# First modulation by column blocks of 1 MB behind x; four q chunks projected chunk by chunk of the tokens in four PSUM banks

## The chip, the core and the metric

The kernel runs on one core of a Trainium2 chip. The core has TensorE (PE in the profile) for matrix products into the accumulation memory PSUM, VectorE (DVE) and ScalarE (ACT) for elementwise work, GpSimd (POOL) and SyncE (SP); each takes its instructions in the order in which they stand, and an instruction that waits holds up everything behind it on its engine. Transfers are issued from a queue of SP, ACT or POOL and are moved by 16 DMA engines that all queues share. The metric is the device time of one execution in microseconds (us), the median of several.

## The reference

One layer of a hybrid diffusion block on 1024 latent tokens and 256 context tokens of width 1024, all in fp32. What this change touches is its beginning: the modulation from the condition `c`, the normed and modulated tokens `h`, and the input projection.

```python
mod = jax.nn.silu(c) @ w_ada[i] + b_ada[i]          # (1, 6 * 1024)
mod_c = jax.nn.silu(c_ctx) @ w_ada[i] + b_ada[i]
sh1, sc1, g1, sh2, sc2, g2 = jnp.split(mod[:, None, :], N_MOD, axis=-1)
hc = modulate(rmsnorm(xc, norm1_g[i]), csh1, csc1)   # x * (1 + scale) + shift
k_c, v_c = jnp.split(hc @ w_in[i][:, NA_WIDTH:3 * NA_WIDTH], 2, axis=-1)
h = modulate(rmsnorm(x, norm1_g[i]), sh1, sc1)
q, k, v, hv, hx1, hx2, gna, ghy = jnp.split(h @ w_in[i], IN_SPLITS, axis=-1)
```

Behind it stand neighbourhood attention on q, k, v (8 heads), a long convolution on hv, hx1, hx2 (with filters from a small sine network), gates, an output projection, and a SwiGLU network; they aren't changed.

## The kernel before

**Products.** An fp32 operand is split into a high part (the value rounded to the fast matmul type, one cast on ACT, line 174) and a low part (the rest, one subtraction on DVE, line 175). A product is then three matmuls: low by high, high by low, high by high (line 194).

**The input projection.** `w_in` has 40 chunks of 128 output columns: 0 to 3 are q, 4 to 7 k, 8 to 11 v, 12 to 23 the convolution's inputs, 24 to 39 the gates. A chunk is projected for two halves of 512 tokens; a half takes 8 contraction chunks by three matmuls, 24 in all, into one PSUM bank (`in_ps`). Chunks 4 to 11 also have a product with the 256 context tokens (`ctx_ps`). `project` is a generator that does one chunk at a time; a priority pulls the next chunk's weights ahead.

**The start** (`hidden`). The first 2048 columns of `w_ada`, 8 MB, are loaded as 8 blocks of 1 MB, each with 128 contraction rows of all columns, in three buffers; every block adds to one accumulation (`ada_ps`, line 299), so that shift and scale are known only when the last block is in. The first four token tiles (x, 128 tokens by 1024) are loaded between the blocks. Their squares are summed on ACT (line 280), the root is taken (line 239), the tiles are scaled (lines 287 and 289), turned on PE (`hT_ps`, line 248), modulated alternately on ACT (line 262) and DVE (line 259) into `htmp`, and split into `hTh` and `hTl`. Tiles 4 to 7 make the second half, the two context tiles `hcTh` and `hcTl`. `filter_hidden` is the sine network (`mlp_ps`, line 338; `farg`, `fkf`, lines 339 to 344; the sine on ACT, line 345), in two layers that stand beside all this.

**What follows.** Three generators are merged by fixed shares: `side` (the filters, lines 350 to 397, then the convolutions) and `proj`, until `side` ends. Then five chunks are projected, and the remaining ones stand between the 32 steps of the attention, one half (24 matmuls) per step; when none is left, `hyena_out` gives 12 matmuls (`hy_ps`) to a step, 16 times. A step is scores (`s_ps`), softmax on DVE and ACT, transposes and the product with v (`pt_ps`), copied out by ACT. The order of all engines' instructions is set when the program is built, by a scheduler that follows priorities and its own estimate of time; lines marked `keep_in_program_order` stay in written order.

These are the lines of the start that set the order:

```python
for k in range(8):
    w = pool.tile([P, 2048], F32, tag="wada", name="wada", bufs=3)
    nc.sync.dma_start(w, a["w_ada"][k, :, 0:2048])
    ...
    if 1 <= k < 5:
        load(k - 1)
    if k == 5:
        normed(0, 4, "rstd1")
```

## Time and profile before

| | |
|---|---|
| time, median of 3 runs | 1698.57 us (1697.81 to 1703.14) |
| the profiled execution's own time | 1693.98 us |
| its span, first to last instruction | 1691.6 us |
| DVE, ACT, POOL busy | 1229.1, 689.6, 153.3 us |
| HBM read and written | 205.48 and 67.39 MB, 161 GB/s over the span |
| granted TensorE clock, mean | 0.994 |

The profile has a page with the busy time of each engine, and views that answer questions on the trace: the timeline (start, duration, engine, line, operation, output<-inputs, number of instructions merged, and in brackets the idle time before it and what ended it) and windows (busy time of each engine in a stretch, then the granted clock, the DMA engines' share and GB/s). Line numbers in them are those of the kernel before. A matmul's shown duration runs to its modelled end; in a row of equal ones the distance from start to start is what one costs. An fp32 product shows as two records.

### The profile page before, as it was taken

What the parts mean: (1) busy time and instruction counts of PE and PEld (TensorE: products, weight loads), DVE (VectorE), ACT (ScalarE), POOL (GpSimd) and SP (SyncE); (2) the same over time, 40 slices, a digit from 0 to 9 for tenths busy, and PEclk for the clock granted to TensorE, in tenths of its full rate; (3) what the DMA queues carried; (4) which work ended last, traced back from release to release, by engine and by line L of the source; (5) the groups of instructions that cost most, each with busy time, mean ns of one, the idle gap of its engine ahead of it and who ended that gap; (6) DMA issues with size and microseconds to landing.
All of it is one profiled execution on the core that took longest, in us unless ns stands there. A gap on an engine that the chain in (4) does not pass through costs nothing.

```text
span 1691.6 us, 22631 instructions
## 1 busy us (share of the span) xinstructions
PE 1645.8 (97%) x8124; PEld 1302.7 (77%) x8124; DVE 1229.1 (73%) x2076; ACT 689.6 (41%) x1206; POOL 153.3 (9%) x274
## 2 busy tenths in 40 slices
PE   6999999999999999999999999999999999999997
PEld 2777667777777787887787887888888888878886
DVE  3799587799986975565866867967865666489467
ACT  4733333222212124545654326733333334355455
POOL 0100210001000022020200001000100111000000
PEclk8999999999999999999999999999999999999999
DMA  9275662655544366344757414333422223395344
GB/s 363 96 241 194 193 215 81 209 168 172 185 169 178 124 204 182 110 140 147 218 159 256 162 62 174 119 129 121 162 92 108 94 102 123 113 359 188 100 119 155
DMA packets 110340, 274.36 MB, mean 162 GB/s; under 512 B 15503, under 2 KB 24595, under 8 KB 107925
## 3 DMA queue, kind: packets, MB, share of 16 engines
q1 hardware_dynamic: 90152, 211.86, 37.3%
q0 software_dynamic: 19280, 60.60, 10.7%
q8 instruction: 64, 1.05, 0.3%
q10 hardware_dynamic: 797, 0.45, 0.1%
q14 instruction: 47, 0.39, 0.1%
HBM read 205.48 MB, written 67.39 MB: 161 GB/s over the span
## 4 chain that ended last, share of the span: by engine, by line
PE 68%; issue 11%; DVE 5%; DMA 3%; ACT 1%; POOL 1%; SPq 0%; DVEq 0%; POOLq 0%; ACTq 0%
PE x_ps L1176 15%; PE in_ps L194 13%; PE z_ps L1176 7%; PE dx_ps L1345 6%; PE out_ps L1114 4%; PE dz_ps L1345 3%; PE dft_ps L447 2%; PE hy_ps L194 2%; PE y_ps L1176 2%; PE pt_ps L805 2%; PE pt_ps L791 2%; PE na_ps L194 2%; PE dy_ps L1345 1%; PE dft_ps L448 1%; PE dft_ps L449 1%
## 5 line engine op out<-in xcount | busy, mean ns | idle before, releaser
L194 PE MATMUL in_ps<-hTh,wl 128*128 128x512 f32 x640 | 258.4, 404 | 0.9 <-ACT proj L619 0.5
L194 PE MATMUL in_ps<-hTl,wh 128*128 128x512 f32 x640 | 252.2, 394 | 0.4 <-DVE hTl L175 0.2
L194 PE MATMUL in_ps<-hTh,wh 128*128 128x512 f32 x640 | 252.2, 394 | 0.0
L194 PEld LDWEIGHTS in_ps<-hTh,wl 128*128 128x128 f32 x640 | 120.5, 188 | 31.3 <-issue 5.3
L194 PEld LDWEIGHTS in_ps<-hTl,wh 128*128 128x128 f32 x640 | 120.6, 188 | 26.5 <-DVE hTl L175 1.9
L194 PEld LDWEIGHTS in_ps<-hTh,wh 128*128 128x128 f32 x640 | 120.5, 188 | 26.6
L175 DVE TENSOR_TENSOR wl<-wr,wh 128x1024 fp32r<-128x1024 f32 (+1 forms) x56 | 59.7, 1067 | 68.4 <-ACT wh L174 68.2
L174 ACT CAST wh<-wr 128x1024 fp32r<-128x1024 f32 (+1 forms) x56 | 51.8, 925 | 139.9 <-PE in_ps L194 112.2
L175 DVE TENSOR_TENSOR ol<-ws,oh 128x512 fp32r<-128x512 f32 x88 | 60.4, 688 | 49.1 <-ACT oh L174 49.0
L175 DVE TENSOR_TENSOR ol<-ar,oh 128x512 fp32r<-128x512 f32 x77 | 52.8, 688 | 48.0 <-ACT oh L174 48.0
L174 ACT CAST oh<-ar 128x512 fp32r<-128x512 f32 x77 | 47.9, 622 | 87.1 <-PE dx_ps L1345 33.1
L174 ACT CAST oh<-ws 128x512 fp32r<-128x512 f32 x88 | 54.7, 622 | 55.7 <-PE x_ps L1176 22.1
L780 ACT ACTIVATE pe<-pe,mx 128x640 f32<-128x640 f32 x64 | 52.6, 823 | 48.7 <-DVE mx L779 48.7
L447 PE MATMUL dft_ps<-a,matf 128*128 128x512 f32 x128 | 66.2, 598 | 4.9 <-issue 2.3
L779 DVE CUSTOM_DVE_ANT_0 pe<-s_ps,bias 128x640 f32<-128x640 f32 x64 | 50.1, 820 | 28.3 <-PE s_ps L774 28.2
L1345 PE MATMUL dx_ps<-ol,oh 128*128 128x512 f32 x176 | 68.7, 390 | 1.7 <-DVE ol L175 1.7
L1345 PE MATMUL dx_ps<-oh,ol 128*128 128x512 f32 x176 | 67.4, 390 | 1.9 <-DVE ol L175 1.9
L1345 PE MATMUL dx_ps<-oh 128*128 128x512 f32 x176 | 68.5, 389 | 0.0
L174 ACT CAST oh<-wr 128x512 fp32r<-128x512 f32 x70 | 43.3, 621 | 51.3 <-PE x_ps L1176 15.5
L175 DVE TENSOR_TENSOR ol<-wr,oh 128x512 fp32r<-128x512 f32 x70 | 48.0, 688 | 22.0 <-ACT oh L174 21.9
L1116 DVE TENSOR_TENSOR x<-x,out_ps 128x512 f32<-128x512 f32 x64 | 42.7, 684 | 16.9 <-PE out_ps L1114 16.7
L895 DVE SCALAR_TENSOR_TENSOR aacc<-wal,cs,aacc 128x512 f32<-128x512 f32 x56 | 41.8, 746 | 17.5 <-DMA wal<-in_w_ada 16.9
(396 smaller groups left out, 4215.8 us busy)
## 6 DMA issues: line engine op xcount, KB each, us to landing
wr<-in_w SPq DMA_DIRECT2D x52, 512.0 KB, 3.4
wr<-in_w_in SPq DMA_DIRECT2D x40, 512.0 KB, 4.4
ar<-g SPq DMA_DIRECT2D x77, 256.0 KB, 3.2
wal<-in_w_ada SPq DMA_DIRECT2D x64, 256.0 KB, 4.1
matf<-in_dft_f SPq DMA_DIRECT2D x32, 384.0 KB, 4.9
bias<-in_rpb SPq DMA_DIRECT2D x64, 192.0 KB, 3.7
g<-t POOLq DMA_DIRECT2D x47, 256.0 KB, 3.1
w<-in_w SPq DMA_DIRECT2D x44, 256.0 KB, 5.4
```

The costliest lines, as they stand in the source:

```text
L174: self.nc.scalar.copy(hi, src)
L175: self.nc.vector.tensor_sub(lo, src, hi.bitcast(F32))
L194: mm = nc.tensor.matmul(ps, ww[:, k * P:(k + 1) * P], xx[:, k, pos:pos + width], start=(i == 0), stop=(i == n - 1))
L447: nc.tensor.matmul(ps, m[:, 0], v.rearrange("p a b -> p (a b)"), start=True, stop=False)
L779: nc.vector.tensor_tensor_reduce(pe, ps[:, 256:896], bt, -1.0, 3e38, ALU.add, ALU.min, mx[:, 0:1])
L780: nc.scalar.activation(pe, pe, AF.Exp, bias=mx[:, 0:1], scale=-1.0, accum_out=mx[:, 1:2])
L791: pin(nc.tensor.transpose(pt[:, at:at + P], pe[:, c * P:(c + 1) * P], self.ident))
L895: nc.vector.scalar_tensor_tensor(acc, w, c, acc, op0=ALU.mult, op1=ALU.add)
L1114: nc.tensor.matmul(ps, gg[x][:, tk], ww[y][:, sl], start=(i == 0), stop=(i == n - 1))
L1116: nc.vector.tensor_add(x1[:, sl], x1[:, sl], ps)
L1176: mm = nc.tensor.matmul(ps, w[u][:, k * P:(k + 1) * P], x[v][:, k, :], start=(start and k == 0 and i == 0), stop=(stop and k == 3 and i == 2),
L1345: nc.tensor.matmul(ps[j], x[u][:, j * P:(j + 1) * P], w[v], start=(start and i == 0 and c == 0), stop=(stop and i == N - 1 and k == len(re ...
```

## The change

`w_ada1` is a second copy of the first 2048 columns, laid out as 8 column blocks of 1 MB: block k has all contraction rows of the 128 shift and the 128 scale columns of chunk k, so one block alone gives shift and scale of that chunk. The four x tiles are loaded first; then come block 0, the weights of q chunk 0, block 1, q chunk 1, and so on, four blocks ahead in the memory of `hT[1]`, all in written order. Each block has 8 small-column matmuls, a copy of 256 columns to SBUF, two matmuls of two columns with a selecting matrix `sel` in place of the transposes, and two small DVE operations. The projection opens with the q chunks 0 to 3, which were 20th to 23rd before: when contraction chunk k of the first half is there, the q chunks add their three matmuls of it, each in its own PSUM bank; q chunk n joins when k reaches n and catches up. The second half goes likewise. Then come 4, 5 and the rest. `left`, which counts the chunks until the last, goes from 40 to 36.

```diff
+    out["w_ada1"] = C(A("w_ada")[0, :, :2 * D].reshape(8, P, 2, 8, P).transpose(3, 1, 0, 2, 4)).reshape(8, P, 2048)
...
-        self.left = 40
+        self.left = 36
...
+    def ada_block(self, pool, psf, w, k, cs, sel):
+        ps = psf.tile([P, 512], F32, tag="f", name="ada_ps")
+        for n in range(8):
+            j = n % 4
+            nc.tensor.matmul(ps[32 * j:32 * j + 32, 0:256], cs[:, n], w[:, n], start=(n < 4), stop=(n >= 4),
+                             tile_position=(0, 32 * j))
+        b = pool.tile([P, 256], F32, tag="msb", name="msb", bufs=2)
+        nc.vector.tensor_copy(b, ps[:, 0:256])
+        for n in range(2):
+            nc.tensor.matmul(ps[:, 256 + 2 * n:258 + 2 * n], b[:, n * P:(n + 1) * P], sel, start=True, stop=True)
...
+        for j in range(4):
+            load(j)
+        for k in range(4):
+            block(k)
+            raws[k] = pool.tile([P, D], F32, tag="x", name="wr", bufs=8)
+            inorder(nc.sync.dma_start(raws[k], a["w_in"][group[k]]))
+        normed(0, 4, "rstd1")
+        turns = [self.turned(psf, xs[0:4], 0)]
         for k in range(8):
...
+            self.ada_block(pool, psf, blocks[k], k, cs, sel)
+            if 1 <= k <= 4:
+                block(k + 3)
+            if k < 7:
+                turns.append(self.turned(psf, xs[0:4], k + 1))
+            self.chunk(pool, turns[k], 4, self.mod1[:, 0], *hT[0], k)
...
+            if k == 6:
+                for j in range(4, 10):
+                    inorder(load(j))
...
         normed(4, 4, "rstd1b")
...
+        for k in range(8):
+            self.chunk(pool, self.turned(psf, xs[4:8], k), 4, self.mod1[:, 0], *hT[1], k)
+            if k == 7:
+                normed(8, 2, "rstd1c")
+            yield
...
+        def opening(group, sts):
+            for h in range(2):
+                banks = [p.tile([P, 512], F32, tag=t, name="in_ps") for p, t in
+                         ((psg[0], "g"), (psg[1], "g"), (psc, "c"), (psf, "f"))]
+                for k in range(8):
+                    next(between)
+                    for n, f in enumerate(group):
+                        if n > k and not h:
+                            continue
+                        wh, wl = self.ready[f]
+                        for kk in (range(k + 1) if n == k and not h else (k,)):
+                            for i, (ww, xx) in enumerate(((wl, 0), (wh, 1), (wh, 0))):
+                                nc.tensor.matmul(banks[n], ww[:, kk * P:(kk + 1) * P], hT[h][xx][:, kk, :],
+                                                 start=(kk == i == 0), stop=(kk == 7 and i == 2))
+                for f, st, pt in zip(group, sts, banks):
+                    out(f, st, [pt], h)
...
-                order = [[4, 5]] + [[f] for f in list(range(6, 24)) + list(range(4)) + list(range(32, 40)) + list(range(24, 30))]
+                order = [list(range(4))] + [[f] for f in list(range(4, 24)) + list(range(32, 40)) + list(range(24, 30))]
```

What the scheduler made of it shows at three places. The first is DVE at the start: `farg` and `fkf` are the sine network, `rstd` the reciprocal that scales x. Before:

```order
L342 SCALAR_TENSOR_TENSOR farg<-fkf,farg 128x1024
L343 SCALAR_TENSOR_TENSOR farg<-fkf,farg 128x1024
L344 TENSOR_SCALAR farg<-farg 128x1024
L241 RECIPROCAL rstd_371<-rstd1s 128x4
L289 TENSOR_SCALAR x<-x,rstd_371 128x1024 x2
```

And now:

```order
L277 TENSOR_REDUCE sel<-ident 128x2
L366 TENSOR_SCALAR fkf<-farg 128x1024
L367 TENSOR_SCALAR fkf<-fkf 128x1024
L368 SCALAR_TENSOR_TENSOR farg<-fkf,farg 128x1024
L369 SCALAR_TENSOR_TENSOR farg<-fkf,farg 128x1024
L242 RECIPROCAL rstd_359<-rstd1s 128x4
L370 TENSOR_SCALAR farg<-farg 128x1024
L296 TENSOR_SCALAR x<-x,rstd_359 128x1024 x2
```

The reciprocal still stands behind the sine network's four long operations; x itself now comes first in the queue of transfers.

The second place is ACT between the two token halves (with buffer numbers; `junk` is the squares of x, here of tiles 4 to 7, `proj` the copies of the finished q chunks out of PSUM):

```order
L265 ACTIVATE htmp_628<-hT_ps_587,mod1_246 128x512
L174 CAST hTh_260<-htmp_628 128x512
L174 CAST hTh_260<-htmp_672 128x512
L287 ACTIVATE junk_676,ssq1_298<-x_632 128x1024
L287 ACTIVATE junk_678,ssq1_298<-x_634 128x1024
L626 ACTIVATE proj_290<-in_ps_294 128x512
L287 ACTIVATE junk_680,ssq1_298<-x_636 128x1024
L626 ACTIVATE proj_291<-in_ps_295 128x512
L287 ACTIVATE junk_682,ssq1_298<-x_638 128x1024
L626 ACTIVATE proj_292<-in_ps_296 128x512
L240 ACT_TABLE_LOAD
L240 ACTIVATE rstd1bs_684<-ssq1_298,eps_236 128x4
```

The first half's last cast (chunk 7) stands ahead of the squares of tiles 4 to 7, as before, where only the cast of one chunk's weights and one copy stood with them; now there are three copies among them.

The third place is PE at the end of the attention (line 826 scores, 846 transposes, 860 the product with v). The last `hy_ps` group now ends like this:

```order
L196 MATMUL hy_ps<-yhh,wh 128x512
L826 MATMUL s_ps<-krh,qrl 128x384 x2
L826 MATMUL s_ps<-krl,qrh 128x384 x2
L826 MATMUL s_ps<-krh,qrh 128x384 x2
L829 MATMUL s_ps<-kch,ql 128x256 x2
L829 MATMUL s_ps<-kcl,qh 128x256 x2
L829 MATMUL s_ps<-kch,qh 128x256 x2
L846 MATMUL pt_ps<-ident,pe 128x128 x10
L860 MATMUL pt_ps<-pts,vc 64x128 x4
L860 MATMUL pt_ps<-pts,v 64x128 x6
```

and before like this:

```order
L194 MATMUL hy_ps<-yhh,wh 128x512
L791 MATMUL pt_ps<-ident,pe 128x128 x10
L805 MATMUL pt_ps<-pts,vc 64x128 x4
L805 MATMUL pt_ps<-pts,v 64x128 x6
L805 MATMUL pt_ps<-pts,vc 64x128 x4
L805 MATMUL pt_ps<-pts,v 64x128 x6
L194 MATMUL na_ps<-yah,wl 128x512
```

Before, 16 attention steps had a projection half beside them and the other 16 a `hy_ps` group, up to the last. Now 10 have a half, 16 a `hy_ps` group, and the last 6 steps follow each other with nothing between.

More of the change, by code (lines that the diff above doesn't have):

```diff
@@ L251, in modulated, with chunk, hidden @@
     def modulated(self, pool, psf, xs, n, mod, hi, lo, raw=None):
+        for k in range(8):
+            self.chunk(pool, self.turned(psf, xs, k), n, mod, hi, lo, k, raw)
+    def chunk(self, pool, pt, n, mod, hi, lo, k, raw=None):
         nc = self.nc
[L254 to L266 removed]
+        h = raw[:, k, :] if raw is not None else pool.tile([P, 512], F32, tag="htmp", name="htmp", bufs=3)
+        if k % 2:
+            nc.vector.tensor_scalar(h[:, :n * P], pt[:, :n * P], mod[:, 0, k:k + 1], mod[:, 1, k:k + 1],
+                                    op0=ALU.mult, op1=ALU.add)
+        else:
+            nc.scalar.activation(h[:, :n * P], pt[:, :n * P], AF.Identity, bias=mod[:, 1, k:k + 1],
+                                 scale=mod[:, 0, k:k + 1])
+        self.split(hi[:, k, :], lo[:, k, :], h[:, :n * P])
+    def hidden(self, pool, wpool, h1, mp, hid, w3, hT, hcT, psf, group):
         nc, a = self.nc, self.a
@@ L294, in hidden @@
             nc.scalar.dma_start(getattr(self, n), a[n])
-        for k in range(8):
-            w = pool.tile([P, 2048], F32, tag="wada", name="wada", bufs=3)
-            nc.sync.dma_start(w, a["w_ada"][k, :, 0:2048])
-            for j in range(4):
-                nc.tensor.matmul(ps[32 * j:32 * j + 32, :], self.cs[:, 2 * k:2 * k + 32], w[:, j * 512:(j + 1) * 512],
-                                 start=(k == 0), stop=(k == 7), tile_position=(0, 32 * j))
-            if 1 <= k < 5:
-                load(k - 1)
-            if k == 5:
-                normed(0, 4, "rstd1")
@@ L305, in hidden @@
[L305 to L313 removed]
+        nc.vector.tensor_scalar(self.bcol[:, 1, :], self.bcol[:, 1, :], 1.0, None, op0=ALU.add)
@@ new lines, in hidden, with block @@
+        for j in range(4):
+            load(j)
+        blocks, raws = [], {}
+        inorder = self.tc.keep_in_program_order
+        def block(k):
+            if k % 2 == 0:
+                w = h1.tile([P, 2, 8, 256], F32, tag="hTl" if k % 4 else "hTh", name="wada")
+                blocks.extend((w[:, 0], w[:, 1]))
+            inorder(nc.sync.dma_start(blocks[k].rearrange("p a b -> p (a b)"), a["w_ada1"][k]))
+        for k in range(4):
+            block(k)
+            raws[k] = pool.tile([P, D], F32, tag="x", name="wr", bufs=8)
+            inorder(nc.sync.dma_start(raws[k], a["w_in"][group[k]]))
@@ L316, in hidden @@
         yield
-        self.modulated(pool, psf, xs[4:8], 4, self.mod1[:, 0], *hT[1])
-        normed(8, 2, "rstd1c")
-        yield
+        hT.append([h1.tile([P, 8, 512], F32R, tag=n, name="hT" + n[-1]) for n in ("hTh", "hTl")])
+        for k in range(8):
+            self.chunk(pool, self.turned(psf, xs[4:8], k), 4, self.mod1[:, 0], *hT[1], k)
+            if k == 7:
+                normed(8, 2, "rstd1c")
+            yield
         self.modulated(pool, psf, xs[8:], 2, self.mod1[:, 1], hcT[0], hcT[1])
@@ L589, in half @@
         def half(f, w, st, ps, h):
-            sl = slice(h * 512, (h + 1) * 512)
             count[0] += 1
@@ L643, in finish @@
                     turn.append((sc, 2, self.vcd.rearrange("(n p) c -> p n c", p=P)[:, :, (f - 8) * P:(f - 7) * P]))
-        for group in groups:
+        def opening(group, sts):
+            for h in range(2):
+                banks = [p.tile([P, 512], F32, tag=t, name="in_ps") for p, t in
+                         ((psg[0], "g"), (psg[1], "g"), (psc, "c"), (psf, "f"))]
+                for k in range(8):
+                    next(between)
[9 more added lines that the diff above has]
+                    out(f, st, [pt], h)
+            for f, st in zip(group, sts):
+                del self.ready[f]
+                finish(f, None, st)
+            next(between)
+        sts = [(self.stg if n < 2 else xpool).tile([P, T], F32, tag="o", name="proj", bufs=2) for n in range(4)]
+        opening(groups[0], sts)
+        for f in groups[1]:
+            self.ready[f] = self.weights(wpool, self.a["w_in"][f], pin=True)
+        yield
+        for group in groups[1:]:
             i = chunks.index(group[-1]) + 1
@@ L661, in project @@
                         yield
-                if group is groups[0]:
-                    next(between)
                 if group is groups[-1] and not h:
```

77 lines of the change are left out of this document (29 added, 48 removed).

## The prediction, made blind

> **What bounds the kernel now.** I read the page first, then the windows, then the timelines of PE, ACT, DVE and SP at the start and at the attention's end.
>
> ```profile
> PE 1645.8 (97%) x8124; PEld 1302.7 (77%) x8124; DVE 1229.1 (73%) x2076; ACT 689.6 (41%) x1206; POOL 153.3 (9%) x274
> ```
> ```profile
> 0.00:10.00 10.00, 3.48 (x4) 1.18 (x4) 0.93 (x3) 1.50 (x2) 1.38 (x7) 1.00 0.81 289
> 10.00:20.00 10.00, 5.77 (x33) 0.91 (x32) 5.34 (x6) 3.25 (x5) 0.00 (x0) 0.85 1.03 420
> 20.00:30.00 10.00, 6.53 (x35) 1.11 (x27) 1.59 (x3) 6.07 (x8) 0.00 (x0) 0.50 1.01 424
> 30.00:40.00 10.00, 8.11 (x57) 5.22 (x50) 5.25 (x13) 5.27 (x9) 0.00 (x0) 0.97 0.81 318
> ...
> 700.00:800.00 100.00, 99.50 (x717) 80.72 (x716) 56.66 (x128) 51.23 (x95) 12.34 (x22) 1.00 0.44 135
> ```
>
> PE is the bound: 97% of the span, 99.5% even beside the attention. So the time is PE's work plus its waits, and a change here is worth the waits that it takes away or makes. They lie mostly in the first 40 us, where transfers run at 420 GB/s and PE waits for the 8 MB of `w_ada`.
>
> ```profile
> 31.49 1.07 PE L299 MATMUL ada_ps<-wada,cs 128*32 128x512 f32 x8
> ...
> 35.82 2.17 PE L248 MATMUL hT_ps<-ident,x 128*128 128x128 f32 x16 [1.24 <-DVE mod L233]
> ...
> 37.75 0.48 PE L194 MATMUL in_ps<-hTh,wl 128*128 128x512 f32 x1
> ...
> 40.33 1.88 PE L338 MATMUL mlp_ps<-feat,mlp 128*128 128x512 f32 x4
> ...
> 68.15 0.39 PE L194 MATMUL in_ps<-hTh,wh 128*128 128x512 f32 x1
> ...
> 70.56 0.89 PE L248 MATMUL hT_ps<-ident,x 128*128 128x128 f32 x6 [0.22 <-ACT htmp L262]
> ...
> 82.54 1.86 PE L367 MATMUL filt_ps<-fw,hid 64*128 64x256 f32 x8 [1.14 <-DVE fv L374]
> ...
> 86.05 0.39 PE L194 MATMUL in_ps<-hTh,wl 128*128 128x512 f32 x1
> ...
> 96.79 0.39 PE L194 MATMUL in_ps<-hTh,wh 128*128 128x512 f32 x1
> ```
>
> The projection begins at 37.75 and has done 96 matmuls (two chunks, both halves) at 68.4. The last two rows are the first and last of 48: 10.74 us over 47 steps, 0.2285 each. The opening now has 192, so the mark to compare with is 68.4 + 96 x 0.2285 = **90.3 us**: when do the opening's 192 end now?
>
> **Step 1: x is ready at 20.0.** Rows of DVE, then ACT:
>
> ```profile
> 13.88 1.22 DVE L343 SCALAR_TENSOR_TENSOR farg<-fkf,farg 128x1024 f32<-128x1024 f32 x1
> ...
> 26.75 0.18 DVE L241 RECIPROCAL rstd<-rstd1s 128x4 f32<-128x4 f32 x1 [10.93 <-ACT rstd1s L239]
> ```
> ```profile
> 15.91 1.06 ACT L345 ACTIVATE feat<-farg 128x1024 f32<-128x1024 f32 x1 [2.02 <-issue]
> ...
> 25.13 1.28 ACT L239 ACT_TABLE_LOAD   x1
> ...
> 26.42 0.30 ACT L239 ACTIVATE rstd1s<-ssq,eps 128x4 f32<-128x4 f32 x1
> ...
> 26.96 2.19 ACT L287 ACTIVATE x<-x,rstd 128x1024 f32<-128x1024 f32 x2 [0.24 <-DVE rstd L241]
> ...
> 32.89 1.05 ACT L174 CAST wh<-wr 128x1024 fp32r<-128x1024 f32 x1
> ...
> 41.66 0.78 ACT L262 ACTIVATE htmp<-hT_ps,mod 128x512 f32<-128x512 f32 x1
> ...
> 42.47 0.62 ACT L174 CAST hTh<-htmp 128x512 fp32r<-128x512 f32 x1
> ...
> 46.72 1.07 ACT L280 ACTIVATE junk<-x 128x1024 f32<-128x1024 f32 x1
> ...
> 47.90 1.06 ACT L280 ACTIVATE junk<-x 128x1024 f32<-128x1024 f32 x1
> ...
> 52.97 0.57 ACT L599 COPY proj<-in_ps 128x512 f32<-128x512 f32 x1
> ```
>
> x (2.1 MB) with the network's tables and `w3` (0.9 MB) is in at 10.3 (2.9 MB in the first 10 us by the window, then 0.42 MB per us); a square step of 1.18 (47.90 less 46.72), table and root give 13.1. But the reciprocal stands behind L343's work, which ends at 15.1 as now; with the small new reduction, 15.3 + 0.2. Then ACT takes, by the order built, one x (1.1), a table (1.28), the sine (1.06) and the last x (1.1): 20.0. Nothing of this moves with the transfers unless the network's tables come earlier; I allow 2 us for that. So 18 us of the head start are gone before a product can be made.
>
> **Step 2: the first half ends at 59.5.** PE's work from 20.0: seven blocks at 1.07 (a block now has twice the matmuls at half the columns; same columns, same price) 7.5; 30 transposes at 2.17/16 = 0.136, 4.1; 96 matmuls 21.9; the network's second layer 1.9. The 16 matmuls with `sel` aren't shown by this trace: at least nothing, at most a transpose each, 2.2; I take 0.1, 1.6. Sum 37.0. Waits, bounded by nothing and 5: until the first `hTh`, ACT needs weights, `htmp`, weights, `hTh` = 1.05 + 0.78 + 1.05 + 0.62 = 3.5, where PE has 2.3 of work; chunk 6's `sel` matmuls stand behind all of chunk 5's, and PE waits about 1.3 for copy, shift, `htmp` and cast. 2.5 in all. The blocks are no bound: block 6 is issued when block 3 is used, about 34 when these rows are laid end to end, and needed at 43; 1 MB takes 2.5 at 0.42 MB per us.
>
> **Step 3: PE waits 9.2 us between the halves.** PE's last 12 matmuls (2.7) can start only with chunk 7's cast, so this cast ends at about 56.6. Behind it ACT has four squares (4.7), three copies (1.7), a table (1.28), the root (0.3): 64.6. Then
>
> ```profile
> 51.88 2.74 DVE L289 TENSOR_SCALAR x<-x,rstd1b 128x1024 f32<-128x1024 f32 x4
> ```
>
> reciprocal and four scalings, 67.5; transposes, `htmp` 0.78, `hTh` 0.62: the second half's first matmul at **69.2**. ACT's table, sine and fourth copy (2.9) fit beside the scalings. PE stands from 59.5 to 69.2 but for four transposes. Before, the same squares ran from 45 to 50 while PE still had 24 and more matmuls.
>
> **Step 4: the opening ends at 97.9.** 96 matmuls and 28 transposes, 25.7; a wait of 1.0 at chunk 6, whose transposes stand behind chunk 5's products; and a cold restart, 2.0:
>
> ```profile
> 28.24 0.90 PE L248 MATMUL hT_ps<-ident,x 128*128 128x128 f32 x3
> ```
>
> Three transposes here took 0.90, 0.30 each against 0.136, at the clock of 0.50 that the window shows; from 30 on it is 0.97, so about 4 us of steady work (from 26.4) brought it back. 4 us at half clock lose 2; the bounds are 0 and 4. The Trainium skill ("TensorE: Matmul & The Clock Gate", Part 1: The HAM clock gate) says that an idle window of about 3.4 us halves the array's clock and about 3.4 us of sustained work restores it; the wait of step 3 is longer than that, and by the page this term would be 1.7. The trace agrees as far as it goes.
>
> Against 90.3 that is **7.6 us late**.
>
> **Step 5: the context tiles, 1.8.** Behind the opening, chunk 4's first matmul needs its weights: ACT has the last copy, two `htmp`, three casts and then the weights,
>
> ```profile
> 69.94 1.02 ACT L262 ACTIVATE htmp<-hT_ps,mod 128x256 f32<-128x256 f32 x2 [0.77 <-PE hT_ps L248]
> ...
> 70.85 1.01 ACT L174 CAST hcTh<-htmp 128x256 fp32r<-128x256 f32 x3
> ```
> ```profile
> 45.32 1.22 DVE L175 TENSOR_TENSOR wl<-wr,wh 128x1024 fp32r<-128x1024 f32 x1
> ```
>
> 0.6 + 1.0 + 1.0 + 1.05, and DVE's subtraction 1.2: 5 us, in which PE has 16 transposes and five small filter products, about 3. Waits 2.5 with those for the last transposes, less the 0.7 that stood here before; bounds 0 and 4.
>
> **Step 6: the filters, 1.4.**
>
> ```profile
> 75.72 0.33 SPq L353 DMA_DIRECT2D rates<-in_rates  x1
> ```
> ```profile
> 81.71 0.68 DVE L374 SCALAR_TENSOR_TENSOR fv<-filt_ps,dec 128x512 f32<-128x512 f32 x1
> ```
>
> From `rates`' issue to the first filter bank read are 6.0. It is issued when the context tiles are split, now some 7.4 behind the opening, so a bank is free at 13.4; PE has work for 11.8. 1.6 and about 0.9 for the next banks, less the 1.14 of before; bounds 0 and 4.
>
> **Step 7: the attention's tail, 2.9.** Three chunks (144 matmuls) left the attention for the start; this pays in steps 2 to 4. Six steps now have no filling.
>
> ```profile
> 870.19 0.44 PE L771 MATMUL s_ps<-krh,qrl 64*128 64x384 f32 x2
> ...
> 873.76 0.51 PE L194 MATMUL hy_ps<-yhh,wl 128*128 128x512 f32 x1
> ...
> 876.73 0.45 PE L771 MATMUL s_ps<-krh,qrl 64*128 64x384 f32 x2
> ...
> 902.81 1.25 PE L791 MATMUL pt_ps<-ident,pe 128*128 128x128 f32 x10
> ...
> 906.86 0.66 PE L805 MATMUL pt_ps<-pts,vc 128*64 128x128 f32 x8 [1.55 <-ACT yrow L812]
> ```
>
> PE's own part of a step is 3.57 (870.19 to 873.76), a filled step 6.54. Unfilled, the transposes must wait for ACT's copies out of their one PSUM tile: 4.05 in the last two steps (902.81 to 906.86). 6 x (4.05 - 3.57) = 2.9; bounds 0, and 17.8 if a step kept its 6.54; I take the row that shows an unfilled step.
>
> **Sum.** 7.6 + 1.8 + 1.4 + 2.9 = 13.7 us later than 1693.98, the profiled execution's own time: 1707.7. The median of the runs shown is 4.6 above that execution, so the forecast for a median is **1712 us**. The middle, 100 to 650 us, keeps its 26 chunks beside the filters and convolutions, and so passes the delay on.
>
> **Rivals.**
> - *No wait between the halves* (the other side). If tiles 4 to 7 are normed when PE gets there, steps 3 and 4 lose 9.2 and 2.0, and the median comes out at 1712 - 11 = 1701, no slower. It decides whether ACT's chunk 7 cast is 13 us ahead of PE's last matmul. For it: x 4 to 7 land by about 46. Against: chunk 7's shift comes from `sel` matmuls that stand behind chunk 6's products on PE, so the cast cannot run ahead. With the low bounds of the other steps as well (13 more) it would be faster, 1688.
> - *PE stays cold through the first half*, since each chunk has small waits. The window 20 to 30 shows 0.50 with PE "busy" 6.53. Ten us more at half clock are 5 lost: 1717. Against: it is 0.97 as soon as PE has steady work. This is the clock page's rule, by which waits under 3.4 us would not do it.
> - *Unfilled attention steps keep 6.54*: 2.9 becomes 17.8, 1727. Against: the tail's rows.
> - *Everything at its low end*: all low bounds (x at 18, no `sel` price, no waits in step 2, no cold restart, steps 5 to 7 at nothing) take 2 + 1.6 + 2.5 + 1.0 + 2.0 + 6.1 = 15 off: 1697.
>
> **Chances.** Forecast (1704 to 1716) 0.62; cold or unfilled steps (above that) 0.14; no wait between the halves, or several low bounds, 0.24, two thirds of it within 0.3%. 0.3%, 5.1 us, is about what a measurement of this kernel can tell from no change: faster is below 1693.5, slower above 1703.7. Slower 0.76, same 0.16, faster 0.08. The range, 1699 to 1722, leaves out the faster case, part of "same", and the longest tail.
>
> **What would show it.** The last x tile scaled at about 20; the first `in_ps` matmul near 23.6; PE idle some 9 us at about 60 to 69, ended by DVE's x (then `htmp`); a clock below 1 just behind; the 192nd matmul near 98; idle before filter products near 110; unfilled attention steps of about 4 us. I am wrong if PE has no gap of over 5 us near 60, if the 192nd matmul ends before 92, or if something behind 115 us gains or loses more than 5 us.

## The result, and the profile after

| | before | changed |
|---|---|---|
| median of 4 runs | 1699.5 us (1697.81 to 1703.14) | 1724.12 us (1714.43 to 1725.76) |
| profiled execution, span | 1693.98, 1691.6 us | 1714.43, 1712.7 us |

The ratio on record is 1.013 with a 95% interval of 1.0089 to 1.0172; it is not that of the two medians, which would be 1.0145. The kernel is slower by 24.6 us at the median, and by 20.5 in the two profiled executions. The direction was as forecast; the size was not. The forecast was 13.4 us above the median of before that it started from (1712 against 1698.57), and 1724 lies 2 us above the end of its range; by the ratio on record, 1698.57 becomes 1720.7, just inside it.

PE's line of the page, then windows of the changed kernel (columns as before: busy time of PE, its weight load, DVE, ACT, POOL, then clock, DMA share, GB/s):

```profile
PE 1657.4 (97%) x8216; PEld 1311.6 (77%) x8216; DVE 1236.7 (72%) x2096; ACT 692.2 (40%) x1207; POOL 153.3 (9%) x274
```
```profile
20.00:30.00 10.00, 9.54 (x75) 5.11 (x68) 5.98 (x12) 5.68 (x7) 0.00 (x0) 1.00 1.01 418
30.00:40.00 10.00, 10.00 (x57) 6.92 (x57) 5.32 (x10) 2.55 (x4) 0.00 (x0) 1.00 0.24 78
...
70.00:80.00 10.00, 5.43 (x13) 3.54 (x13) 3.79 (x7) 5.62 (x7) 0.00 (x0) 0.50 0.00 0
...
700.00:800.00 100.00, 96.02 (x671) 77.80 (x671) 58.16 (x134) 52.44 (x97) 12.45 (x22) 0.98 0.47 141
```

PE is busy 11.6 us longer than before (1657.4 against 1645.8), and the rest of the loss is idle time. From 30 on transfers are no limit any more (a share of 0.24, where the kernel before had 0.81), and still PE is busy without a break. The page alone would pass for a kernel at its bound; only the timeline shows what PE is busy with. PE's rows in the first half, at the gap, and at the end of the opening:

```profile
17.80 0.66 PE L249 MATMUL hT_ps<-ident,x 128*128 128x128 f32 x2 [7.69 <-DVE x L296]
...
19.79 1.93 PE L227 MATMUL ada_ps<-wada,csp 128*32 128x256 f32 x14
...
22.96 1.07 PE L227 MATMUL ada_ps<-wada,csp 128*32 128x256 f32 x16
...
25.69 0.50 PE L688 MATMUL in_ps<-hTh,wl 128*128 128x512 f32 x1 [0.25 <-ACT hTh L174]
...
45.49 0.62 PE L227 MATMUL ada_ps<-wada,csp 128*32 128x256 f32 x2
46.04 0.61 PE L232 MATMUL ada_ps<-sel,msb 128*128 128x2 f32 x4
46.58 1.06 PE L227 MATMUL ada_ps<-wada,csp 128*32 128x256 f32 x14
47.57 0.66 PE L249 MATMUL hT_ps<-ident,x 128*128 128x128 f32 x4
...
50.82 0.63 PE L227 MATMUL ada_ps<-wada,csp 128*32 128x256 f32 x6
51.38 0.51 PE L688 MATMUL in_ps<-hTl,wh 128*128 128x512 f32 x1
...
66.76 0.40 PE L688 MATMUL in_ps<-hTh,wh 128*128 128x512 f32 x1
72.55 1.05 PE L249 MATMUL hT_ps<-ident,x 128*128 128x128 f32 x2 [5.39 <-DVE x L296]
...
76.44 2.08 PE L688 MATMUL in_ps<-hTh,wl 128*128 128x512 f32 x4 [1.52 <-ACT hTh L174]
...
104.95 0.39 PE L688 MATMUL in_ps<-hTh,wh 128*128 128x512 f32 x1
```

Three things are to be seen. A block of `w_ada` is eight matmuls, two records each: all 16 together take 1.07 (22.96), and 14 take 1.06, or 1.0 until the next work starts (46.58 to 47.57), while the two records put ahead by the scheduler take 0.55 by themselves (45.49 to 46.04). The block's matmuls go to four column positions, and the times read as if up to four ran side by side: one alone and three (six records, 50.82 to 51.38) both take about half a microsecond, seven and eight take 1.0, so that a lone one makes three rounds out of two. Second, the gap: the first half ends at 67.0, and the second begins at 76.4, with a clock of 0.50. Third, the opening ends at 105.2, **14.9 us behind the mark of 90.3**.

To follow the delay on, I take the same product in both traces and subtract 0.2285 us for each `in_ps` product that now stands ahead of it. This lag is 14.9 at the opening's end, 11.5 at the first scores of the attention (the first `s_ps` product), 18.6 at the first product behind it (`na_ps`) and 21.1 at the last product of all. So the attention is the second place. It hands over from `in_ps` to `hy_ps` at its step 10 now (16 before), and that step takes 12.2 us where the others with `hy_ps` take 6.5. PE, then ACT and SP there:

```profile
785.15 0.45 PE L826 MATMUL s_ps<-krh,qrl 64*128 64x384 f32 x2
...
792.84 0.50 PE L196 MATMUL hy_ps<-yhh,wl 128*128 128x512 f32 x1 [3.33 <-ACT proj L649]
...
793.88 0.63 PE L196 MATMUL hy_ps<-yhh,wl 128*128 128x512 f32 x1
794.31 0.63 PE L196 MATMUL hy_ps<-yhl,wh 128*128 128x512 f32 x1
...
797.38 0.45 PE L826 MATMUL s_ps<-krh,qrl 64*128 64x384 f32 x2
```
```profile
791.88 0.40 ACT L174 CAST kch<-kcraw 128x256 fp32r<-128x256 f32 x1 [4.99 <-DMA kcraw<-kc]
792.20 0.59 ACT L649 ACTIVATE proj<-in_ps 128x512 f32<-128x512 f32 x1
```
```profile
785.61 1.08 SPq L776 DMA_DIRECT2D kcraw<-kc  x2
```

PE waits for ACT's copy out of `in_ps`, whose bank `hy_ps` takes. ACT is idle: the copy stands behind a cast that waits 5 us for the raw context keys of the next pair of heads. Behind the 3.3 us wait PE's products come 0.43 apart (793.88 to 794.31) instead of 0.23 for a while.

### The profile page after: what moved, and what is told of

Read it like the earlier page. It is cut to its first block, busy times and chain, and to the rows that moved or that the text cites. A ratio compares the mean times of both kernels' runs of the same rounds, so it can differ in the third digit from the quotient of the medians.

```text
span 1712.7 us, 22819 instructions
## 1 busy us (share of the span) xinstructions
PE 1657.4 (97%) x8216; PEld 1311.6 (77%) x8216; DVE 1236.7 (72%) x2096; ACT 692.2 (40%) x1207; POOL 153.3 (9%) x274
## 3 DMA queue, kind: packets, MB, share of 16 engines
q8 instruction: 65, 1.06, 0.3%
## 4 chain that ended last, share of the span: by engine, by line
PE 72%; issue 10%; DVE 8%; DMA 6%; ACT 3%; POOL 1%; ACTq 0%; SPq 0%; DVEq 0%; POOLq 0%
PE x_ps L1230 15%; PE in_ps L196 12%; PE z_ps L1230 7%; PE dx_ps L1399 5%; PE out_ps L1168 5%; PE dz_ps L1399 3%; PE hy_ps L196 3%; PE in_ps L688 3%; PE dft_ps L473 3%; PE na_ps L196 3%; PE y_ps L1230 2%; PE pt_ps L846 2%; PE pt_ps L860 2%; PE dft_ps L474 1%; PE dft_ps L475 1%
## 5 line engine op out<-in xcount | busy, mean ns | idle before, releaser
L196 PE MATMUL in_ps<-hTh,wl 128*128 128x512 f32 x576 | 232.9, 404 | 1.5 <-ACT proj L649 1.3
L196 PE MATMUL in_ps<-hTh,wh 128*128 128x512 f32 x576 | 228.0, 396 | 0.0
L196 PE MATMUL in_ps<-hTl,wh 128*128 128x512 f32 x576 | 227.3, 395 | 0.0
L196 PEld LDWEIGHTS in_ps<-hTh,wl 128*128 128x128 f32 x576 | 108.5, 188 | 27.8 <-issue 3.5
L196 PEld LDWEIGHTS in_ps<-hTh,wh 128*128 128x128 f32 x576 | 108.4, 188 | 24.2 <-issue 1.0
L196 PEld LDWEIGHTS in_ps<-hTl,wh 128*128 128x128 f32 x576 | 108.5, 188 | 22.2 <-issue 0.3
L174 ACT CAST wh<-wr 128x1024 fp32r<-128x1024 f32 (+1 forms) x56 | 51.8, 925 | 118.9 <-PE in_ps L196 90.3
L174 ACT CAST oh<-ws 128x512 fp32r<-128x512 f32 x88 | 54.7, 622 | 58.4 <-PE x_ps L1230 28.7
L834 DVE CUSTOM_DVE_ANT_0 pe<-s_ps,bias 128x640 f32<-128x640 f32 x64 | 50.2, 820 | 20.6 <-PE s_ps L829 20.5
L1170 DVE TENSOR_TENSOR x<-x,out_ps 128x512 f32<-128x512 f32 x64 | 42.6, 685 | 15.9 <-PE out_ps L1168 15.7
L950 DVE SCALAR_TENSOR_TENSOR aacc<-wal,cs,aacc 128x512 f32<-128x512 f32 x56 | 41.9, 749 | 16.7 <-DMA wal<-in_w_ada 16.1
```

The lines of the kernel that those rows point to most:

```text
L174: self.nc.scalar.copy(hi, src)
L196: mm = nc.tensor.matmul(ps, ww[:, k * P:(k + 1) * P], xx[:, k, pos:pos + width], start=(i == 0), stop=(i == n - 1))
L834: nc.vector.tensor_tensor_reduce(pe, ps[:, 256:896], bt, -1.0, 3e38, ALU.add, ALU.min, mx[:, 0:1])
L950: nc.vector.scalar_tensor_tensor(acc, w, c, acc, op0=ALU.mult, op1=ALU.add)
L1170: nc.vector.tensor_add(x1[:, sl], x1[:, sl], ps)
```

## The experiments

Times are compared with runs of the kernel before on the same chip; the column "above before" is the difference of the medians. The executions of one kernel differ by up to 13 us (run 7: 1699.0 to 1712.0), so the rows of a trace often say more than the time; but each trace shows one execution. Lags as above; the opening's end in us.

| run | above before | ratio, 95% interval | opening's end | lag at first scores | lag behind the attention |
|---|---|---|---|---|---|
| changed kernel | 24.6 | 1.0130 (1.0089 to 1.0172) | 105.2 | 11.5 | 18.6 |
| again | 22.9 | 1.0135 (1.0103 to 1.0168) | 105.4 | 16.0 | 25.2 |
| early squares | 10.5 | 1.0057 (1.0035 to 1.0080) | 96.3 | 6.7 | 12.2 |
| late table | 24.1 | 1.0139 (1.0108 to 1.0170) | 109.4 | 20.0 | 26.2 |
| written order | 14.9 | 1.0096 (1.0064 to 1.0129) | 100.3 | 7.6 | 16.1 |
| two halves ahead | 19.6 | 1.0114 (1.0083 to 1.0144) | as changed | 19.2 | 20.8 |
| blocks alone | 11.6 | 1.0063 (1.0041 to 1.0086) | (other order) | 16.1 | 16.1 |
| early + order | 4.2 | 1.0032 (1.0012 to 1.0052) | 91.1 | 5.1 | 13.1 |
| all four | 7.5 | 1.0045 (1.0029 to 1.0061) | 90.8 | 0.8 | 2.8 |
| early + order, filled | 11.6 | 1.0067 (1.0045 to 1.0089) | 88.9 | 10.7 | 9.8 |
| keys' buffer | 17.1 | 1.0108 (1.0080 to 1.0135) | as changed | 14.2 | 17.5 |
| early + order + warm | 6.7 | 1.0037 (1.0021 to 1.0054) | 88.1 | -4.3 | 2.6 |
| the same + keys' buffer | 2.3 | 1.0017 (1.0001 to 1.0033) | 88.4 | -1.2 | -0.2 |

**1. The changed kernel again** (no edit).

> The changed kernel once more. Its profiled execution took 1714.4 us and its other three 1723 to 1726, 10 us more, with a granted clock of 0.992 against 0.994, which alone is 3.4 us. If the start, the attention and the slow drift of 4 us between 1100 and 1490 are the kernel's own, a second profile shows them again: last product of the first half at 67, a gap of 9.4 us, the opening's end at 105, 12.2 us in the attention step that hands over from in_ps to hy_ps, and about 1% more per product between 1100 and 1490 than before's trace has. If the 10 us are one more wait that some executions have, one of these rows differs in this profile; if they are the chip's pace, only the spacing of products does. Times 1714 to 1726.

The profiled execution took 1724.1 us, 10 more than the first. The opening is the same to 0.3 us (gap 9.4, end 105.4). The difference lies in several places, none of them over 5 us: 4.5 more by the first scores, most of it between 110 and 300, 13.5 instead of 12.2 at the handover, and 3.1 behind the attention. So the 10 us are not one wait. The stretch of 1146 to 1461, in which PE is never idle, shows the pace, in windows of before and then of this run:

```profile
1146.00:1461.00 315.00, 315.00 (x1391) 260.85 (x1390) 204.87 (x318) 116.25 (x200) 32.42 (x60) 1.00 0.32 110
```
```profile
1146.00:1461.00 315.00, 315.00 (x1377) 258.44 (x1376) 214.74 (x333) 115.24 (x198) 32.92 (x61) 1.00 0.33 114
```

The profiled execution of before did 1391 products in it, this one 1377, 1% fewer. By the same products, the work that took before 314.8 us takes 318.1 in this profile, in the first one of the changed kernel, and in the profiles of all the runs below, alike to 0.1 us. Whether these 3.3 us belong to that one execution of before or to the changed program is open: the kernel before was profiled once.

**2. Early squares.** The raw weights take the first of the eight `x` buffers, so that x tiles 4 to 7 come into buffers that are free early.

```diff
+        raws = {k: pool.tile([P, D], F32, tag="x", name="wr", bufs=8) for k in range(4)}
         for j in range(4):
             load(j)
...
+            if k == 4:
+                for j in range(4, 8):
+                    inorder(load(j))
+            if k in (5, 6):
+                squares(2 * k - 6, 2)
             if k == 6:
-                for j in range(4, 10):
+                normed(4, 4, "rstd1b")
+                for j in range(8, 10):
                     inorder(load(j))
...
-        normed(4, 4, "rstd1b")
```

> x tiles 4 to 7 get the buffers of the raw weights, are loaded at chunk 4 and squared, rooted and scaled between chunks 5 and 7, so ahead of the first half's end. Theory (the wait between the halves is worth its length): the gap falls from 9.4 us to under 3, the clock does not fall to 0.50 behind it, the opening ends 8 to 11 us earlier (about 95 instead of 105), and the kernel is 8 to 11 us faster than the changed one: about 1713 by its median, or 1705 by its profile. Rival (the middle of the kernel soaks it up, as it regained about 3 us between 110 and 330): the opening ends 8 to 11 earlier, but the attention begins under 4 us earlier, and the time is within 4 us of the changed kernel's.

Windows of this run:

```profile
60.00:70.00 10.00, 8.74 (x35) 5.39 (x34) 8.06 (x15) 5.80 (x11) 0.00 (x0) 1.00 0.20 77
70.00:80.00 10.00, 9.93 (x55) 8.22 (x54) 7.61 (x10) 6.90 (x10) 0.00 (x0) 1.00 0.01 2
```

The gap and the clock of 0.50 are gone, at the price of a first half that ends 2.2 us later (DVE's scalings stand in it). The opening ends 8.9 earlier and the kernel is about 12 us faster than the changed one. The theory holds: the wait between the halves was worth its length and what the cold array lost behind it. The rival falls.

**3. Late table.** The sine network's first layer stands behind chunk 1; one small DVE addition moves behind the scaling of x with it.

```diff
-        next(mlp)
...
+            if k == 1:
+                next(mlp)
```

> The sine network's first layer is put behind chunk 1; nothing else. Theory (the head start was lost to DVE's and ACT's work for the network, which stands ahead of the reciprocal and the last scaled x tile): the reciprocal runs at 14.6 instead of 16.2, x is scaled at about 17 instead of 20.9, the first in_ps stands at 21 to 22 instead of 25.7, and the first half ends 3 to 4 us earlier, as does the kernel. Rival (chunk 0 waits for w_ada's blocks or raw weights, or PE is cold anyway): the first in_ps moves by less than 1.5 us and the first half still ends at 66 to 67.

The rival held at the start. The reciprocal ran at 15.9 (x itself landed 1.3 us later here), all of x was scaled at 18.3 instead of 20.9, and the first `in_ps` stood at 25.7, where it was. But the moved network's own products (1.4 us at 23.9 and 25.2) now stood ahead of it, so this does not show what x's readiness alone is worth. The network's work between the chunks also made a wait of 2.4 at 36, and the first half ended at 70.4, later than the theory or the rival had it.

**4. Written order.** In the first half all of PE's products are pinned: `sel` of chunk k, the block of k+1 whole, the transposes of k+1, the products of k-1.

```diff
+            next(ada[k])
+            if k < 7:
+                ada.append(self.ada_block(pool, psf, blocks[k + 1], k + 1, cs, sel))
+                next(ada[k + 1])
...
+                if not h:
+                    next(between)
```

> In the first half every product of PE stands in one written order: a block's eight matmuls together and one chunk ahead, the two sel matmuls between the product groups, the products one chunk behind. Theory (the first half lost 7.5 us to PE's own work: a matmul of the next block put ahead by itself costs 0.55 us, so that a block takes 1.6 instead of 1.07): the first half ends at 62 to 63 instead of 67, with no lone ada matmul, and the kernel is about 4 us faster than the changed one. Rival (the price is that of any change from one kind of product to another, or PE waits for DVE and ACT in their chains whatever the order): the lone matmuls are gone, but idle time or longer sel groups take their place, and the first half ends within 1.5 us of 67.

One chunk on PE:

```profile
46.68 0.50 PE L234 MATMUL ada_ps<-sel,msb 128*128 128x2 f32 x4
47.11 1.07 PE L228 MATMUL ada_ps<-wada,csp 128*32 128x256 f32 x16
48.12 0.66 PE L252 MATMUL hT_ps<-ident,x 128*128 128x128 f32 x4
48.53 0.48 PE L697 MATMUL in_ps<-hTh,wl 128*128 128x512 f32 x1
...
51.40 0.50 PE L234 MATMUL ada_ps<-sel,msb 128*128 128x2 f32 x4
```

`sel` 0.43, block 1.0, transposes 0.4, twelve products 2.9: 4.72 us from chunk to chunk. From the first `in_ps` (28.0) to the end of the half (63.9) this takes 35.9 us, against 41.3 in the changed kernel. The half starts 2.3 later, since the pinned transposes wait 2.15 us for the fourth x tile, and still ends 3.1 earlier; the median difference fell by 8.0 us. The two stretches do not hold quite the same work: a block more (1.0 us) stands ahead of the first product here. So about 4.4 us of the first half were the price of the order in which PE met its small products.

**5. Two halves ahead.** `AHEAD = 5` becomes 2.

> The changed kernel with two half projections instead of five ahead of the attention, so that three more of its steps have filling and the handover from in_ps to hy_ps falls on step 13 instead of 10. Theory (the attention's loss is a collision: at step 10 a new pair's keys are prepared, their kcraw load shares two buffers and the SP queue with the eight yhraw loads, and ACT's cast of it stands ahead of the copy that frees PE's bank): the handover step takes about 7 us instead of 12.2, three steps of 3.6 to 4.1 are filled, and the attention's share is 5 to 6 us less. Rival (it starts too early: the first steps' keys and values are not ready without the three halves, 16 us): the handover is short, but the first steps wait as much or more, and the time is within 2 us of the changed kernel's, or above. Second rival (handing over costs 12 at any step): step 13 takes 12.

The handover step (13, the one with the first `hy_ps` product) took 6.5 us like those behind it, so handing over does not cost 12 at any step, and the theory's 7 held. But the first scores waited 3.5 us and ran at half pace. Lag from 15.7 ahead of that wait to 20.8 behind the attention: 5.1, against 7.1 and 9.2 in the two profiles of the changed kernel. The time does not tell it from the changed kernel.

**6. Blocks alone.** The new modulation without the new order: the four raw weights, the opening and the q chunks in front are taken out, the projections go as before (4 and 5, then 6 to 23, then q), with 40 chunks' steps left.

```diff
-                order = [list(range(4))] + [[f] for f in list(range(4, 24)) + list(range(32, 40)) + list(range(24, 30))]
+                order = [[4, 5]] + [[f] for f in list(range(6, 24)) + list(range(4)) + list(range(32, 40)) + list(range(24, 30))]
```

> One part of the change alone: the modulation by column blocks behind x, with before's order of the projections (chunks 4 and 5 first, then one by one, q behind v), no products between the modulation's chunks, and 40 chunks' steps left as before. Theory (the new modulation is ready sooner and only the products woven into it, and the gap that they cause, lose time): the eight chunks are modulated by about 37 to 40, the first in_ps stands at 36 or before (37.75 in the kernel before), tiles 4 to 7 are squared while PE has products, the 96th product ends at 60 to 64 instead of 68, and the kernel is 3 to 8 us faster than the kernel before, about 1692. Rival (column blocks cost PE and the chain of shift, htmp and cast as much as the rows did): the 96th product is at 68 or behind it, and the time 1698 or more.

Far from the theory, and past the rival. PE, then DVE:

```profile
35.42 0.61 PE L232 MATMUL ada_ps<-sel,msb 128*128 128x2 f32 x4 [1.47 <-DVE msb L230]
...
39.12 0.61 PE L232 MATMUL ada_ps<-sel,msb 128*128 128x2 f32 x4 [1.50 <-DVE msb L230]
...
42.78 0.61 PE L232 MATMUL ada_ps<-sel,msb 128*128 128x2 f32 x4 [1.47 <-DVE msb L230]
```
```profile
38.03 0.69 DVE L175 TENSOR_TENSOR hTl<-htmp,hTh 128x512 fp32r<-128x512 f32 x1 [1.56 <-ACT hTh L174]
38.64 0.42 DVE L230 COPY msb<-ada_ps 128x256 f32<-128x256 f32 x1
```

From the fifth chunk on a chunk takes 3.7 us even with no products between, because DVE's copy of the next block stands behind the subtraction of this chunk, which waits for ACT's cast. The first `in_ps` stands at 50.1 (37.75 before), the 96th at 82.5 (68.15): 14.4 us late, as late as the changed kernel's opening, with the products not woven in at all. The attention then costs nothing (16.1 ahead of it and behind it). So the modulation by blocks alone loses as much as the opening loses, but not in the same way: here PE waits for the chain of a chunk, while in the changed kernel it is idle for 1.2 us of the first half. That the two amounts are alike says nothing of a common cause. For the attention the reading is firmer: without the move of three chunks out of it, its loss is gone.

**7. Early squares and written order together.**

> Both edits of the start together: tiles 4 to 7 squared early, and PE's written order in the first half. Theory (they take different losses: one the wait between the halves, 9.4 us, the other the lone matmuls inside the first half): the gains of 12.4 and 8.0 us by the medians add in the main; the opening ends at 91 to 93, the kernel at 1701 to 1705. Rival (both take the same wait, since a first half that ends sooner makes the gap longer): the opening ends at 95 to 96 as with the squares alone, and the time is 1707 to 1710.

They add: the opening ends at 91.1, 0.8 behind the mark, and the kernel is 4.2 us above before, at 1702.5. In the trace the attention is the largest part of what is left: 7.9 of the 13.1 us of lag behind it.

**8. All four**: this with the late table and two halves ahead.

> As the run with both edits of the start, with the network's first layer behind chunk 1 and two half projections ahead of the attention. Theory: with PE's order written out the first transposes no longer wait for the fourth x tile behind the network's sine, so the first in_ps stands at 23 to 25 instead of 28, and the handover is short: 1694 to 1699, the time of the kernel before. Rival (the network's work inside the first half costs there what it gave at the start, and the attention starts too early): 1701 to 1705, as without these two.

The opening gained 0.3 us (the first `in_ps` at 27.7); blocks still took 1.93 until 25. The profile, of the fastest of its nine executions, has a lag of 2.8 us behind the attention, but the median is 1705.8, and no better than without the two. Inconclusive in time; of the late table it says no again.

**9. Early + order, filled.** Three chunks stay for the attention.

```diff
-                    yield
+                    yield 1 if f < 24 else 1.75
```

> The kernel with both edits of the start, and the single-chunk projections behind chunk 23 counted 1.75 times in the merge with the filters and convolutions, so that three chunks stay for the attention: 16 of its steps have in_ps filling and 16 hy_ps, as in the kernel before. Theory (what is left behind the opening is the attention's: handover at a step that also prepares keys, and six unfilled steps): the attention from its first to its last scores takes 246 us as before (7 to 10 us less than now, net of the work moved), the 16th step's handover about 7 us, and the kernel is 6 to 9 us faster than with the two edits: 1694 to 1697, so no slower than the kernel before. Rival (the convolutions need those three chunks as filling, which is what they had in both kernels): the attention is short again, but the stretch from 400 to 650 loses 3 us or more, and the time is 1700 to 1703.

The rival held, larger than it said. The attention lost nothing (lag 10.7 ahead, 9.8 behind), but the last convolutions lost 10.7 us between 563 and 627, in a window of this run:

```profile
563.00:627.00 64.00, 57.33 (x212) 41.06 (x212) 58.78 (x100) 12.32 (x20) 2.15 (x4) 0.89 0.40 140
```

DVE is busy 92% there, and PE, without products to fill in, waits and falls to a clock of 0.89. Three chunks of filling are missing in one place or in the other.

**10. Keys' buffer.**

```diff
-            x = self.stg.tile([P, 4, P], F32, tag="tm", name="kcraw")[:, 0:2].rearrange("p a b -> p (a b)")
+            x = prep.tile([P, 512], F32, tag="raw", name="kcraw", bufs=2)[:, 0:TC]
```

> The changed kernel, with the raw context keys (kcraw) in the buffers of the raw queries instead of the two that yhraw uses; every step in its place. Theory (at the handover kcraw's load waits for a yhraw buffer, and ACT's queue with the copy of in_ps behind its cast waits for that load): the load is issued before 782 instead of at 785.6, ACT's idle time of 5.0 us ahead of the cast falls under 2, PE's idle time ahead of the first hy_ps falls from 3.3 to under 1, and the handover step takes 8 to 9 us instead of 12.2. Rival (it is yh or the gates that come late, or the bank): the cast runs early, and the first hy_ps product still waits 3 us or more, for yhl or ghy.

The load is issued at 729.9 and its cast done at 762.1, long before the handover. That step took 8.6 us instead of 12.2, and PE no longer waited for ACT's copy of `in_ps`; 2.0 us of wait for the copy of `yrow` were left in it, which stood behind casts of late yhraw loads. Lag across the attention 3.3 us (14.2 to 17.5) instead of 7.1. In the seven profiles that hand over at step 10 without this edit, the step took 10.2 to 13.5 us; with it, 8.6 here and 6.7 in run 12. The median difference is 17.1 us, 6 to 8 less than in the two runs of the changed kernel.

**11. Warm**: 32 products of the identity with itself, read by nobody, ahead of the first block.

```diff
+        wp = psf.tile([P, 512], F32, tag="f", name="warm_ps")
+        for _ in range(32):
+            inorder(nc.tensor.matmul(wp[:, 0:P], self.ident, self.ident, start=True, stop=True))
```

> The kernel with both edits of the start, and 32 products of the identity with itself on PE ahead of the first w_ada block, between 10 and 15 us, when PE is idle; their result is read by nobody. Theory (PE runs at half pace at the start since it was idle before: blocks take 1.93 us until 28 against 1.07 behind, which the prediction's second step left out): blocks take 1.07 from the first one that stands behind x, the first in_ps stands at 24.5 to 25.5 instead of 27.9, and the first half ends 2.5 to 3.5 us earlier, at about 61. Rival (the pace comes from elsewhere, as the granted clock of the window says 1.00; or DVE's and ACT's chains set it): blocks stay at 1.93 until about 28, or the first in_ps moves by under 1 us.

PE's rows without them (run 7), then with them:

```profile
21.70 1.93 PE L228 MATMUL ada_ps<-wada,csp 128*32 128x256 f32 x16
...
25.26 1.93 PE L228 MATMUL ada_ps<-wada,csp 128*32 128x256 f32 x16
...
27.89 0.78 PE L706 MATMUL in_ps<-hTh,wl 128*128 128x512 f32 x1
```
```profile
9.30 9.23 PE L328 MATMUL warm_ps<-ident 128*128 128x128 f32 x64
18.46 1.07 PE L228 MATMUL ada_ps<-wada,csp 128*32 128x256 f32 x16
...
25.26 0.48 PE L709 MATMUL in_ps<-hTh,wl 128*128 128x512 f32 x1
```

Blocks take 1.07 from the first one, though it now stands 4 us later (18.46, against 14.10 in run 7); the first product comes 2.6 earlier, and the half ends 3.0 earlier. That the pace comes from idle time ahead holds for the trace; the size of the gain is less sure. Run 9 starts as run 7 does, and its rows are:

```profile
21.51 1.93 PE L228 MATMUL ada_ps<-wada,csp 128*32 128x256 f32 x16
...
24.75 1.07 PE L228 MATMUL ada_ps<-wada,csp 128*32 128x256 f32 x16
...
26.16 0.48 PE L706 MATMUL in_ps<-hTh,wl 128*128 128x512 f32 x1
```

So between two executions of one start the half pace ends at different times. Against run 9 the extra products gain 0.9 us at the first product and 0.8 at the opening's end (88.1 against 88.9). In the time they show nothing (6.7 above before, against 4.2 in run 7). By its lags the trace leads before by 4.3 us at the attention, where that of run 7 was 5.1 behind; the profiled execution of run 7 was the slowest of its ten.

**12. The same with the keys' buffer.**

> All that helped so far in one kernel: tiles 4 to 7 squared early, PE's written order and its 32 extra products at the start, and the context keys' own buffers; the order of the projections as in the changed kernel. Theory (the losses are separate and add): the opening ends at 88, the handover step takes 8 to 9 us instead of 12.7, the attention costs about 6 us net of the moved work, and the kernel is 3 to 4 us faster than the one without the keys' buffers: 1699 to 1701, still 1 to 3 us behind the kernel before, since the six unfilled steps stay. Rival (what the start gains is lost between 110 and 650, as the extra products' 3 us at the opening showed nothing in the time): 1702 to 1704. Second rival: the opening's lead of 6 to 8 us over the kernel before reaches the end, and the time is below 1697.

The handover step took 6.7 us, and the lag across the attention was 1.0. The median is 2.3 us above before, 4.4 less than without the buffers: the theory by the difference, the first rival by the absolute time, and the interval (1.0001 to 1.0033) does not settle it. No version of the change was faster than the kernel before.

## Why the prediction was right, and where its sizes were off

By its own terms, on the axis of the profiled execution; the two measured columns are the two profiles of the changed kernel:

| term | forecast | measured | again |
|---|---|---|---|
| steps 1 to 4, opening | 7.6 | 14.9 | 15.1 |
| steps 5 and 6, until the attention | 3.2 | -3.4 | 0.9 |
| step 7, attention | 2.9 | 7.1 | 9.2 |
| behind it | 0 | 2.6 | 5.6 |
| sum | 13.7 | 21.1 | 30.8 |

The direction was no luck: the two losses that carry it, the opening and the attention, were forecast as losses. Both were mis-sized, by a factor of two to three, and that the sum is not further off owes something to steps 5 and 6.

**Step 1** was right: DVE's sine work stood ahead of the reciprocal, the last x tile was scaled at 20.9 (20.0). Whether this was the bound of the start stays open: run 3 took it away and the first product stayed at 25.7, behind 1.4 us of the network's own products.

**Step 2 was mis-sized**, 59.5 against 67.0, and this is nearly all of the opening's error of 7.3. The prediction listed PE's work at warm prices and in whole groups. From its first transposes at 17.8, behind a wait of 7.69 us, until about 22 PE ran at half pace (14 records of a block took 1.93 at 19.8, 16 took 1.07 at 23.0). Four microseconds at half pace lose an estimated 2.0, about the 2.1 by which the first product was late (25.7, not 23.6); but x was 0.9 late as well, and run 11 got 0.9 to 2.6 us back at this place by keeping PE busy ahead of it. The price of a block was taken from the row at 31.49, while the trace of before has the cold price too:

```profile
15.30 1.06 PE L299 MATMUL ada_ps<-wada,cs 128*32 128x512 f32 x8 [1.55 <-DMA wada<-in_w_ada]
19.04 1.93 PE L299 MATMUL ada_ps<-wada,cs 128*32 128x512 f32 x8 [2.67 <-DMA wada<-in_w_ada]
22.70 1.93 PE L299 MATMUL ada_ps<-wada,cs 128*32 128x512 f32 x8 [1.72 <-DMA wada<-in_w_ada]
```

The rest is the order: between first product and end the half took 41.3 us, where the forecast had 35.9 and run 4, with whole blocks, took 35.9 (with one block moved ahead of the first product, 1.0). `sel` cost 0.43 per chunk in that order, not 0.2. The waits, priced at 2.5, were only 1.2: the scheduler filled them with lone matmuls, which cost more than the wait. The rival "PE stays cold through the first half" was right only for its first 4 us. The argument against it, that waits under 3.4 us would not do it, does not hold in this case: in the rows above no wait is over 2.67 us, and the block's time still goes from 1.06 to 1.93, with a clock of 0.50 in the window 20 to 30.

**Steps 3 and 4 were right**: the gap is 9.4 us (9.7 by the forecast's times) with the releasers as named, and from the second half's first product to the opening's end are 28.7 us (28.7), with 1.08 at chunk 6. Run 2 shows that the gap is worth its length and what follows it. The Trainium skill ("TensorE: Matmul & The Clock Gate", Part 1: The HAM clock gate) puts the cold restart at 3.4 us of work; the trace agrees: products came 0.43 apart from 76.4 until 80.0. By the same section of the Trainium skill an array that has been idle for about 3.4 us is cold; the wait of 7.69 us ahead of the first transposes was longer than that, and the forecast used the rule for the gap and not for the start. The rival without a wait between the halves fell with the gap.

**Steps 5 and 6** were too small to be told: -3.4 in one execution, 0.9 in the other.

**Step 7 failed in its mechanism.** It priced unfilled steps, and these were right (3.6 for the first, 4.05 to 4.2 for the next four; forecast 4.05). It missed that the handover from `in_ps` to `hy_ps` moves to a step that also prepares keys, where ACT's in-order queue joins the two (5.1 us more than the handover of before; the keys' buffer takes 3.6 us off the step in run 10, and 6.0 in run 12). By the prediction's own sign of being wrong, a loss of over 5 us behind 115, this part was wrong. "The middle passes the delay on" was about right (14.9 in, 11.5 out, and 15.1 in, 16.0 out), and run 9 shows what it rests on: the middle needs its 26 chunks.

One lesson was in no rival: by run 6 the new modulation is 14.4 us late without any products woven in. The forecast compared the opening with PE's work and never asked how long the chain of one chunk (block, copy, `sel`, shift, `htmp`, cast, subtraction) is through two in-order engines. In the changed kernel PE is idle for only 1.2 us of the first half, so there the woven products cover this chain. Settled as places are the gap, the written order, the handover and the cold start; the prices of the first three are shown within a few us, that of the cold start only as 0.9 to 2.6. Open is why the last version's lead at the opening (1.9 us by 88.4 against 90.3) comes out as 2.3 us behind in the time. Its trace shows two places that were not tried: between 245 and 445 the lag goes from -7.7 to -0.6, and behind the attention it goes from -0.2 to 6.9, of which 3.3 are the stretch of run 1 in which all these profiles are slower than the one of before.

## What to carry to other kernels

Count small products by visits and not by columns: a group that the scheduler split as one and seven cost 1.55 us here instead of 1.0, and in a stretch where PE is "busy" this shows only in the spacing of its rows. Before products that fill waits are moved, ask what they cover now, and look at every seam that moves with them: which prefetch shares buffers and an in-order queue with it there. And time the chain of one step of a new pipeline through all its engines before anything is woven into it.

## What the hardware showed unexpectedly

- The granted clock is 1.00 in the changed kernel's window 20 to 30, and in its window 10 to 20, while 14 records of a block take 1.93 us there that take 1.0 later: the column does not show the start's half pace; the spacing does.
- A lone matmul of a block (weights of 32 columns) costs 0.55 us between other products, as much as three of them at different column positions; eight take 1.0.
- Two products with 2 columns each take 0.36 to 0.54 us in the changed kernel's first half once its pace is full, about as much as four transposes of 128 columns (0.4 to 0.6).
- With PE never idle and a granted clock of 1.00, the pace still differed by 1% between the one profile of before and all thirteen of the changed kernel and its versions (1391 and 1377 products in 315 us); what makes the difference is not shown.
